# Attention value products with both precision parts in one 512-column pass

## The chip, the cores and the metric

The kernel runs on one core of a Trainium2 chip. Its time is the device time in microseconds (us) of one execution; the time before is the median of three. A profile of one execution shows what each engine did: PE multiplies matrices (a matmul streams the columns of a moving operand past stationary weights, which a separate weight load, PEld, brings in), DVE and ACT do elementwise work and are the only ones here that read PE's results out of PSUM, POOL does elementwise work in SBUF, SP starts transfers. PSUM is cut into banks, and one bank holds 512 float32 columns on 128 partitions.

## The reference

One layer of a hybrid decoder on 1024 tokens of width 1024: RMSNorm, one input projection, 8 heads of causal attention beside 4 heads of a gated recurrence, an output projection, then a gated MLP. What the change touches is the attention:

```python
s = jnp.where(valid[None, :, None, None], s, -jnp.inf)
m = jnp.max(s, axis=-1)
p = jnp.exp(s - m[..., None])
l = jnp.sum(p, axis=-1)
o = jnp.einsum('bnqrhe,...', p.astype(v.dtype), vw)   # weights times values
...
return (num / den[..., None])[:, :S]
```

The three dilation patterns are merged into one softmax per query with an additive mask, so each head is a causal attention of 1024 queries by 1024 keys with 64 columns per head.

## The kernel before, in words

Products at float32 accuracy are made of several products in fp32r: each operand x is split into a high part hi (a rounding copy) and a low part lo = x - hi, and hi*hi, hi*lo and lo*hi are added up in PSUM.

The attention stage runs from about 57 to 298 us. It goes through heads h = 0 to 7, in each through query pairs j = 0 to 3 (256 queries, two blocks A and B of 128), and in each through key pairs i = 0 to j (256 keys). Scores (`score_steps`): PE makes a score bank S of up to 512 keys (L585, L586, two buffers), DVE adds the mask and takes it out into P with the row's minimum (L588), ACT takes the exponential with the row's sum (L593), DVE the reciprocal (L594), POOL scales P (L597). Where a row has more than 512 keys, L592 joins the two minima on DVE. Values (`value_steps`): `tr` transposes four 128x128 blocks of P into one bank T (L612 to L619, two buffers; three blocks on the diagonal, i = j), ACT copies T to the high part (L623), DVE makes the low part from T (L624). `pv` multiplies: the stationary operand is the value tile v with the 64 high columns and the 64 low columns of V beside each other, so that rows 0 to 63 of the result O hold the products with V's high part and rows 64 to 127 those with its low part; the moving operand is the high, then the low part of the transposed weights. That makes four matmuls per tile, two for each block of 128 keys, all adding into columns 0 to 255 of one bank. `end` adds the two halves of the rows: ACT copies rows 64 to 127 to `ot` (L639), DVE adds rows 0 to 63 (L641). There are 48 full tiles and 32 diagonal ones, and 32 ends.

PE's order is written out by the program (the engine is scheduled by hand). Beside the attention it does projection work in portions that `Fill` hands out: the next head's q and k (`qk_half`, products `p__qk`), then value and recurrence projections (`pV`, `piv`). The evacuation of q and k is on DVE (`x`, L549, then L552, L553, L555) and ACT (L550, L551). The order of DVE, ACT and POOL is chosen by a scheduler at build time from its own costs; only instructions given to `pin` keep their program order among each other, and the sums in `end` are among these. Each engine works its own queue strictly in order, so an instruction that waits holds up all behind it.

## Time and profile before

| | |
|---|---|
| median of three runs | 1208.58 us (1207.88 to 1208.98) |
| the profiled execution's own time | 1207.86 us |
| its span in the profile | 1205.9 us |
| PE busy | 1192.7 us, 99% of the span, 6014 matmuls |
| PE weight loads | 1005.6 us, 83% |
| DVE, ACT, POOL busy | 947.8 (79%), 631.4 (52%), 298.5 us (25%) |
| chain that ended last | PE 95%, DVE 3%, ACT 1% |

A busy share says how full an engine is on average; which wait ends last is read in the timeline of the place. The profile gives each matmul a duration that runs over into the following ones, because matmuls are pipelined: steps between starts, not durations, say what PE's time costs. TensorE's granted clock was at full speed in the stretches shown below.

### The profile page before, as it was taken

To read this page: it belongs to the slowest core of one execution; us is meant where nothing else is said; L and a number is where in the kernel's file an instruction comes from. 1 tells how busy PE (TensorE), PEld (TensorE's weight loads), DVE (VectorE), ACT (ScalarE), POOL (GpSimd) and SP (SyncE) were. 2 spreads that over 40 slices of the span, in tenths; PEclk is the share of its full clock that TensorE was granted. 3 is DMA by queue.
4 is the path that set the end of the run, shared out by engine and by line. 5 is a ranking of instruction groups with operands and counts; after the bars stand their busy time and mean duration, and the time that the engine had idled before them with its cause. 6 is when DMAs were issued, how large, how long until landed. Compare 5 with 4: busy or idle time off the path is not lost.

```text
span 1205.9 us, 17474 instructions
## 1 busy us (share of the span) xinstructions
PE 1192.7 (99%) x6014; PEld 1005.6 (83%) x6014; DVE 947.8 (79%) x1783; ACT 631.4 (52%) x1217; POOL 298.5 (25%) x276
## 2 busy tenths in 40 slices
PE   9999999999999999999999999999999999999996
PEld 8988888888888888888888888888888888888886
DVE  8767776666778776484999899898888978957986
ACT  8766666667666565454643343433443444444553
POOL 1154446544001014413231322312223200000000
PEclk9999999999999999999999999999999999999999
DMA  7021112223111123432113323333223267534532
GB/s 273 10 71 54 53 54 88 64 65 120 36 36 54 60 64 112 133 125 94 42 64 114 108 85 106 121 116 109 84 98 122 96 213 249 156 98 158 166 103 89
DMA packets 71833, 122.39 MB, mean 101 GB/s; under 512 B 7360, under 2 KB 17856, under 8 KB 71744
## 3 DMA queue, kind: packets, MB, share of 16 engines
q1 hardware_dynamic: 60528, 101.41, 26.3%
q10 hardware_dynamic: 11216, 19.86, 4.3%
q8 instruction: 47, 0.77, 0.3%
q14 instruction: 42, 0.34, 0.1%
HBM read 97.65 MB, written 23.59 MB: 101 GB/s over the span
## 4 chain that ended last, share of the span: by engine, by line
PE 95%; DVE 3%; ACT 1%; issue 0%; POOL 0%; DVEq 0%; ACTq 0%
PE p L1132 11%; PE p L1133 11%; PE p L1134 11%; PE ds L1433 3%; PE ds L1431 3%; PE ds L1432 3%; PE po L1036 2%; PE po L1038 2%; PE po L1037 2%; PE da L1433 2%; PE da L1431 2%; PE da L1432 2%; PE piv L512 1%; PE piv L514 1%; PE piv L513 1%; PE S L585 1%
## 5 line engine op out<-in xcount | busy, mean ns | idle before, releaser
L88 POOL TENSOR_TENSOR wlo<-raww,whi 128x512 fp32r<-128x512 f32 x141 | 208.6, 1491 | 382.4 <-ACT whi L86 231.6
L86 ACT CAST whi<-raww 128x512 fp32r<-128x512 f32 x276 | 167.7, 617 | 183.9 <-DVE raww L120 69.1
L88 DVE TENSOR_TENSOR wlo<-raww,whi 128x512 fp32r<-128x512 f32 x136 | 97.5, 717 | 22.8 <-ACT whi L86 22.7
L86 ACT CAST whi<-r 128x512 fp32r<-128x512 f32 x70 | 43.6, 623 | 83.1 <-PE ds L1432 51.3
L597 POOL TENSOR_SCALAR P<-P,st 128x512 f32<-128x512 f32 (+2 forms) x96 | 55.8, 592 | 107.9 <-DVE st L594 50.5
L588 DVE CUSTOM_DVE_ANT_0 P<-S,mask 128x512 f32<-128x512 f32 (+2 forms) x96 | 52.0, 553 | 29.9 <-PE S L586 28.9
L593 ACT ACTIVATE P<-P,st 128x128 f32<-128x128 f32 (+3 forms) x64 | 49.7, 777 | 32.0 <-DVE st L588 16.7
L88 DVE TENSOR_TENSOR wlo<-r,whi 128x512 fp32r<-128x512 f32 x70 | 47.9, 685 | 20.0 <-ACT whi L86 19.9
L624 DVE TENSOR_TENSOR tl<-T,th 128x512 fp32r<-128x512 f32 (+1 forms) x80 | 50.8, 634 | 16.2 <-ACT th L623 15.1
L1433 PE MATMUL ds<-fhi,wlo 128*128 128x512 f32 x160 | 62.3, 389 | 0.0
L1432 PE MATMUL ds<-flo,whi 128*128 128x512 f32 x160 | 62.3, 389 | 0.0
L1431 PE MATMUL ds<-fhi,whi 128*128 128x512 f32 x160 | 62.2, 389 | 0.0
L1132 PE MATMUL p<-b1h,whi 128*128 128x512 f32 x160 | 62.2, 389 | 0.0
L1133 PE MATMUL p<-b1l,whi 128*128 128x512 f32 x160 | 62.2, 389 | 0.0
L1134 PE MATMUL p<-b1h,wlo 128*128 128x512 f32 x160 | 62.2, 389 | 0.0
L1161 ACT ACTIVATE cv<-cv 128x512 f32<-128x512 f32 x44 | 27.9, 633 | 61.5 <-DVE cv L1154 61.4
L1154 DVE SCALAR_TENSOR_TENSOR cv<-g,vec,cv 128x511 f32<-128x511 f32 (+2 forms) x92 | 56.1, 615 | 4.7 <-ACT cv L1151 3.7
L1405 POOL TENSOR_TENSOR facc<-facc,sqf 128x256 f32<-128x256 f32 x2 | 1.5, 738 | 223.7 <-ACT sqf L1404 223.7
L623 ACT CAST th<-T 128x512 fp32r<-128x512 f32 (+1 forms) x80 | 43.0, 537 | 23.4 <-PE T L616 20.3
L86 ACT CAST fhi<-rawf 128x512 fp32r<-128x512 f32 x70 | 43.2, 617 | 15.2 <-DMA rawf<-spT 7.0
L88 DVE TENSOR_TENSOR flo<-rawf,fhi 128x512 fp32r<-128x512 f32 x70 | 47.9, 684 | 3.6 <-ACT fhi L86 3.6
L1431 PE MATMUL da<-fhi,whi 128*128 128x512 f32 x120 | 46.7, 389 | 0.0
(672 smaller groups left out, 3832.5 us busy)
## 6 DMA issues: line engine op xcount, KB each, us to landing
raww<-in_w_up_dram SPq DMA_DIRECT2D x88, 256.0 KB, 3.1
raww<-in_w_tok_dram SPq DMA_DIRECT2D x52, 256.0 KB, 2.7
rawf<-spT SPq DMA_DIRECT2D x40, 256.0 KB, 2.7
r<-in_w_down_dram SPq DMA_DIRECT2D x40, 256.0 KB, 3.5
raww<-in_w_hg_dram SPq DMA_DIRECT2D x32, 256.0 KB, 2.6
raww<-in_w_out_dram SPq DMA_DIRECT2D x32, 256.0 KB, 2.6
spB<-a ACTq DMA_DIRECT2D x30, 256.0 KB, 2.2
spT<-t ACTq DMA_DIRECT2D x30, 256.0 KB, 2.0
```

What stands on the lines that cost most here:

```text
L86: self.pin(self.high(hi[:, :w], raw))
L88: self.pin(low.tensor_sub(lo[:, :w], raw, f32(hi[:, :w])))
L588: DVE.tensor_tensor_reduce(Pt[:, k0 : k0 + w], S[:, :w], mask[:, m : m + w], -1.0, BIG * 3, op0=ALU.add, op1=ALU.min, accum_out=st[:, k0 / ...
L597: POOL.tensor_scalar(e, e, st[:, 3:4], 1.0, op0=ALU.mult, op1=ALU.mult)
L624: DVE.tensor_sub(tl[:, :n], T[:, :n], f32(th[:, :n]))
L1132: PE.matmul(ps, hi[:, s], bhi, start=(start and n == 0), stop=False)
L1133: PE.matmul(ps, hi[:, s], blo, start=False, stop=False)
L1134: PE.matmul(ps, lo[:, s], bhi, start=False, stop=(stop and n == len(rhs) - 1))
L1154: DVE.scalar_tensor_tensor(dst, x, col(V_CW + j * NFF + f), dst, op0=ALU.mult, op1=ALU.add)
L1431: PE.matmul(ps[d], hi[:, s], ahi, start=(k == 0), stop=False)
L1432: PE.matmul(ps[d], hi[:, s], alo, start=False, stop=False)
L1433: PE.matmul(ps[d], lo[:, s], ahi, start=False, stop=(k == NPAIR - 1))
```

## The change

High and low part of the transposed weights now lie in one tile `t` of shape 128 x 2 x 512. `pv` streams the two parts in one pass: a moving operand of two runs of 256 columns, one from each part, into a bank seen as two halves, so that the high part's products land in columns 0 to 255 and the low part's in 256 to 511. On the diagonal the second key block goes with two runs of 128 columns into columns 128 to 255 and 384 to 511. A tile takes two matmuls where it took four; the columns that are streamed stay the same. `end` adds three things: ACT copies rows 64 to 127 of the first half as before, DVE adds rows 0 to 63 of the second half to `ot`, then rows 0 to 63 of the first half. The rows 64 to 127 of the second half (low part of V times low part of the weights) are left out of the sum, where the kernel before had them in it. Two early weight tiles that borrow the tags of `th` and `tl` borrow the new one.

```diff
--- before.py
+++ after.py
@@ -369,7 +369,8 @@
     TB = 3
 
     def aside(i):
-        return tuple(at.tile([P, H2], F32R, tag=x, name=f"{x}w{i}", bufs=TB) for x in ("th", "tl"))
+        t = at.tile([P, 2, H2], F32R, tag="t", name=f"tw{i}", bufs=TB)
+        return t[:, 0], t[:, 1]
 
     ring.aside = {(("qk", 1), i): aside for i in range(2)}
     ring.aside["a12", 1] = None
@@ -618,26 +619,27 @@
                 else:
                     PE.transpose(T[:, 256:384], B[:, k1], ident)
                     n = 384
-                th = at.tile([P, H2], F32R, tag="th", name=f"th{h}_{j}_{i}", bufs=TB)
-                tl = at.tile([P, H2], F32R, tag="tl", name=f"tl{h}_{j}_{i}", bufs=TB)
-                ACT.copy(th[:, :n], T[:, :n])
-                DVE.tensor_sub(tl[:, :n], T[:, :n], f32(th[:, :n]))
-                parts[i] = th, tl
+                t2 = parts[i] = at.tile([P, 2, H2], F32R, tag="t", name=f"t{h}_{j}_{i}", bufs=TB)
+                ACT.copy(t2[:, 0, :n], T[:, :n])
+                DVE.tensor_sub(t2[:, 1, :n], T[:, :n], f32(t2[:, 0, :n]))
 
             def pv(i):
-                th, tl = parts.pop(i)
+
+                t2 = parts.pop(i)
                 last = i == j
                 v0, v1 = V[:, 2 * i, h % 4, :], V[:, 2 * i + 1, h % 4, :]
-                PE.matmul(O[:, 0:256], v0, th[:, 0:256], start=(i == 0), stop=False)
-                PE.matmul(O[:, 0:256], v0, tl[:, 0:256], start=False, stop=False)
-                o_, m_ = (O[:, 0:256], slice(256, 512)) if not last else (O[:, 128:256], slice(256, 384))
-                PE.matmul(o_, v1, th[:, m_], start=False, stop=False)
-                PE.matmul(o_, v1, tl[:, m_], start=False, stop=last)
+                o2 = O.rearrange("p (x q) -> p x q", x=2)
+                PE.matmul(o2, v0, t2[:, :, 0:256], start=(i == 0), stop=False)
+                if last:
+                    PE.matmul(o2[:, :, 128:256], v1, t2[:, :, 256:384], start=False, stop=True)
+                else:
+                    PE.matmul(o2, v1, t2[:, :, 256:512], start=False, stop=False)
 
             def end():
                 ot = at.tile([64, 256], F32, tag="ot", name=f"ot{h}_{j}", bufs=2)
                 ACT.copy(ot, O[64:128, 0:256])
                 r0 = 64 * (h % 2)
+                pin(DVE.tensor_add(ot, O[0:64, 256:512], ot))
                 pin(DVE.tensor_add(raw[h // 2, j // 2][r0 : r0 + 64, (j % 2) * 256 : (j % 2 + 1) * 256], O[0:64, 0:256], ot))
 
             for i in range(j + 1):
```

The build-time scheduler also orders DVE, ACT and POOL anew. Two places on DVE are shown, each before and after. In the names, a trailing number is a tile's serial number; `ot_3` and `raw_1` belong to the end of query pair 3 of the head before, `ot_0` and `raw_0` to that of pair 0; `P_6` is the row block 6 of the scores with its two evictions.

The first place is DVE in head 3, from the split of the next head's q and k to the evictions of row block 6. Before:

```order
L592 TENSOR_TENSOR st_5_1889<-st_5_1889 128x1
L553 SCALAR_TENSOR_TENSOR qs_1894<-x_0_1896,qs_1894 64x512
L555 TENSOR_TENSOR kl_204<-x_0_1896,kh_1895 64x512
L594 RECIPROCAL st_5_1889<-st_5_1889 128x1
L641 TENSOR_TENSOR raw_1_562<-O_3_1687,ot_3_1923 64x256
L624 TENSOR_TENSOR tl_1_1_1931<-T_1_1_1926,th_1_1_1930 128x384
L641 TENSOR_TENSOR raw_0_561<-O_0_1835,ot_0_1950 64x256
L588 ISA P_6_1953,st_6_1954<-S_6_0_1955,mask 128x512
L588 ISA st_6_1954 128x1
```

After:

```order
L556 TENSOR_TENSOR kl_202<-x_0_1815,kh_1814 64x512
L595 RECIPROCAL st_5_1808<-st_5_1808 128x1
L642 TENSOR_TENSOR ot_3_1840<-O_3_1621,ot_3_1840 64x256
L624 TENSOR_TENSOR t_1_1_1848<-T_1_1_1844,t_1_1_1848 128x384
L643 TENSOR_TENSOR raw_1_560<-O_3_1621,ot_3_1840 64x256
L642 TENSOR_TENSOR ot_0_1865<-O_0_1758,ot_0_1865 64x256
L589 ISA P_6_1869,st_6_1870<-S_6_0_1871,mask 128x512
L589 ISA st_6_1870 128x1
L643 TENSOR_TENSOR raw_0_559<-O_0_1758,ot_0_1865 64x256
L589 ISA P_6_1869,st_6_1870<-S_6_512_1875,mask 128x384
```

Ahead of the first eviction of `P_6` stood two sums (`raw_1`, `raw_0`); now three stand there (`ot_3`, `raw_1`, `ot_0`), and the fourth (`raw_0`) between the two evictions.

The second place is DVE in head 2, near the end of row block 7, with the evacuation `x_1` of the next head's projection. Before:

```order
L588 ISA st_7_1588 128x1
L592 TENSOR_TENSOR st_7_1588<-st_7_1588 128x1
L594 RECIPROCAL st_7_1588<-st_7_1588 128x1
L624 TENSOR_TENSOR tl_2_1_1618<-T_2_1_1612,th_2_1_1617 128x512
L549 TENSOR_TENSOR x_1_1645<-p__qk___3_1_1509,R_89 128x512
L641 TENSOR_TENSOR raw_0_561<-O_1_1481,ot_1_1634 64x256
L624 TENSOR_TENSOR tl_2_2_1642<-T_2_2_1637,th_2_2_1641 128x384
L552 CAST kh_1501<-x_1_1645 64x512
```

After:

```order
L593 TENSOR_TENSOR st_7_1529<-st_7_1529 128x1
L550 TENSOR_TENSOR x_1_1581<-p__qk___3_1_1454,R_89 128x512
L595 RECIPROCAL st_7_1529<-st_7_1529 128x1
L624 TENSOR_TENSOR t_2_1_1556<-T_2_1_1551,t_2_1_1556 128x512
L642 TENSOR_TENSOR ot_1_1570<-O_1_1427,ot_1_1570 64x256
L624 TENSOR_TENSOR t_2_2_1578<-T_2_2_1574,t_2_2_1578 128x384
L643 TENSOR_TENSOR raw_0_559<-O_1_1427,ot_1_1570 64x256
L553 CAST kh_1446<-x_1_1581 64x512
```

The evacuation `x_1` now stands ahead of the reciprocal of row block 7 and of the lo part `t_2_1`, and the sums of pair 1 have grown from one to two. On ACT the copy `ot_3` has moved ahead of the copies that follow `x_0` (L550, L551), and `ot_0` behind a weight cast (L86). On PE nothing is moved but the merged products.

## Rows read from the trace of the kernel before

**Rows 1.** Busy time in the attention stage. Columns: stretch in us and its length, then for PE, weight loads, DVE, ACT and POOL the busy us with the number of instructions, then the granted clock of TensorE as a share of full speed, the share of the DMA engines and GB/s.

```profile
57.00:298.00 241.00, 238.67 (x1473) 210.15 (x1471) 162.38 (x442) 161.61 (x333) 128.50 (x152) 1.00 0.22 68
```

**Rows 2.** Waits of PE from 57 to 300 us, the row of the score products: who waited, for whom, us in total, times, longest.

```profile
PE S L585 <- DVE st L588: 0.8, 2, 0.4
```

**Rows 3.** Groups of instructions by line and shape: the last product of a tile in its two shapes, which tell the full tiles (48) from the diagonal ones (32), and from the view of one line the sum that ends a query pair (duration in ns: least, median, most).

```profile
L635 PE MATMUL O<-tl,v 128*128 128x256 f32 x48 | 13.6, 283 | 0.0
...
L635 PE MATMUL O<-tl,v 128*128 128x128 f32 x32 | 8.8, 275 | 0.0
...
L641 DVE TENSOR_TENSOR raw<-O,ot x32: 396/417/419, 58.7 to 298.7; 64x256 f32<-64x256 f32 x32
```

**Rows 4.** Timeline of PE in head 3 (columns of every timeline: start, us taken, engine, line, instruction, output and inputs, shape, and in brackets an idle time before it with what ended it). What counts is the step from one start to the next, since the ends run over into the next instruction. First a 512-column step; then a diagonal tile (first product at 146.03) up to the second product of the work behind it; then a full tile (first product at 153.58) up to the work behind it.

```profile
145.33 0.40 PE L460 MATMUL p__qk___4_1_1903<-ulo,whi 128*128 128x512 f32 x1
145.56 0.39 PE L461 MATMUL p__qk___4_1_1903<-uhi,wlo 128*128 128x512 f32 x1
...
146.03 0.28 PE L631 MATMUL O<-th,v 128*128 128x256 f32 x1
...
146.43 0.45 PE L458 MATMUL p__qk___4_1_1903<-uhi,whi 128*128 128x512 f32 x1
146.72 0.40 PE L460 MATMUL p__qk___4_1_1903<-ulo,whi 128*128 128x512 f32 x1
...
153.58 0.28 PE L631 MATMUL O<-th,v 128*128 128x256 f32 x1
...
154.06 0.39 PE L458 MATMUL p__qk___4_1_1903<-uhi,whi 128*128 128x512 f32 x1
```

**Rows 5.** The same timeline at the stop of head 3 near 151.9 us: DVE, then ACT, then PE.

```profile
144.81 0.69 DVE L624 TENSOR_TENSOR tl<-T,th 128x512 fp32r<-128x512 f32 x1 [0.64 <-ACT th L623]
...
149.34 0.17 DVE L594 RECIPROCAL st<-st 128x1 f32<-128x1 f32 x1
149.56 0.42 DVE L641 TENSOR_TENSOR raw<-O,ot 64x256 f32<-64x256 f32 x1
150.07 0.56 DVE L624 TENSOR_TENSOR tl<-T,th 128x384 fp32r<-128x384 f32 x1
150.66 0.42 DVE L641 TENSOR_TENSOR raw<-O,ot 64x256 f32<-64x256 f32 x1
151.10 0.69 DVE L588 CUSTOM_DVE_ANT_0 P<-S,mask 128x512 f32<-128x512 f32 x1
...
149.16 0.37 ACT L639 COPY ot<-O 64x256 f32<-64x256 f32 x1
...
150.06 0.37 ACT L639 COPY ot<-O 64x256 f32<-64x256 f32 x1
...
151.86 0.50 PE L585 MATMUL S<-kh,qs 128*128 128x512 f32 x1 [0.38 <-DVE st L588]
```

**Rows 6.** Timeline some 6 us before the end of a head, in head 2: DVE from the reciprocal of row block 7 to the lo part of the fourth query pair's first key pair (131.02), then PE's last product of the next head's projection and the transposes of the fourth pair's third key pair, which take the bank that this lo part has read.

```profile
125.80 0.16 DVE L594 RECIPROCAL st<-st 128x1 f32<-128x1 f32 x1 [1.37 <-ACT P L593]
126.28 0.69 DVE L624 TENSOR_TENSOR tl<-T,th 128x512 fp32r<-128x512 f32 x1 [0.31 <-ACT th L623]
126.88 0.68 DVE L549 TENSOR_TENSOR x<-p__qk___3_1_1509,R 128x512 f32<-128x512 f32 x1
127.48 0.41 DVE L641 TENSOR_TENSOR raw<-O,ot 64x256 f32<-64x256 f32 x1
127.81 0.54 DVE L624 TENSOR_TENSOR tl<-T,th 128x384 fp32r<-128x384 f32 x1
...
131.02 0.69 DVE L624 TENSOR_TENSOR tl<-T,th 128x512 fp32r<-128x512 f32 x1
...
125.62 0.40 PE L461 MATMUL p__qk___3_1_1509<-uhi,wlo 128*128 128x512 f32 x1
...
131.81 0.28 PE L612 MATMUL T<-ident,P 128*128 128x128 f32 x1
```

**Rows 7.** Timeline, the like places of other heads: the score products at 121, 182 and 282 us, the transposes at 102 and 193 us, then DVE's second score eviction of row block 6 in head 7 (281.68), and the place of rows 6 in head 5 (the transposes on PE, the lo part on DVE).

```profile
101.52 0.33 PE L612 MATMUL T<-ident,P 128*128 128x128 f32 x1
...
121.37 0.50 PE L585 MATMUL S<-kh,qs 128*128 128x512 f32 x1
...
182.19 0.50 PE L585 MATMUL S<-kh,qs 128*128 128x512 f32 x1
...
192.56 0.33 PE L612 MATMUL T<-ident,P 128*128 128x128 f32 x1
...
281.82 0.50 PE L585 MATMUL S<-kh,qs 128*128 128x512 f32 x1
...
282.39 0.40 PE L585 MATMUL S<-kh,qs 128*128 128x512 f32 x1
...
281.68 0.55 DVE L588 CUSTOM_DVE_ANT_0 P<-S,mask 128x384 f32<-128x384 f32 x1
...
227.05 0.27 PE L612 MATMUL T<-ident,P 128*128 128x128 f32 x1
...
225.89 0.67 DVE L624 TENSOR_TENSOR tl<-T,th 128x512 fp32r<-128x512 f32 x1
```

**Rows 8.** Two groups from the view of one line, in the later recurrence stage: L892 streams the same 64 columns twice over (a moving operand in two runs), L891 streams 128 columns in one run. Durations in ns: least, median, most.

```profile
L892 PE MATMUL psA<-E,B x64: 272/273/323, 327.1 to 475.7; 128*64 128x128 f32 x64
...
L891 PE MATMUL psA<-E,B x64: 272/273/324, 327.1 to 475.7; 128*64 128x128 f32 x64
```

## The prediction

> **What bounds the kernel now.** I began with the busy times: PE is at 99% of the span, and in the attention stage, the only stretch that the change touches, at 238.67 of 241 us, with DVE at 162.4, ACT at 161.6 and POOL at 128.5 [rows 1]. The reader sees one full engine, so time that PE saves is time saved, but only where nothing else makes PE late. So I read PE's waits next: those of the score products for DVE add up to just 0.8 us, in two places [rows 2]. That view lists only clear idle time. The timeline shows more: the same score product, the first of row block 7, starts late in each of heads 1 to 4 and in head 7, after the step before it or with a duration of 0.50 instead of 0.40 us [rows 5, 7]. It needs the bank that DVE's eviction of row block 6 has just left, and DVE comes to that eviction through a run of work without gaps from 144.81 on [rows 5]. A second place is nearly as tight: the transposes at 131.81 us take the bank that a lo part left at 131.02 + 0.69 = 131.71, and at 101.52 and 193 us they even start with a small wait (0.33 instead of 0.28 us) [rows 6, 7]. Last I compared how the two programs stand on each engine, to see what DVE has in front of those two places now.
>
> **PE's saving.** A full tile's four products step from 153.58 to 154.06, 0.48 us [rows 4]. Two products of 512 columns take two steps like that from 145.33 to 145.56, 0.23 each, together 0.46. With starts rounded to 0.01 the gain is 0.01 to 0.02; I take 0.015, and 48 tiles [rows 3] give 0.7 us. On the diagonal the gain is larger, because of the 128-column products: from the first product at 146.03 to the second product of the work behind it, at 146.72, are 0.69 us [rows 4]; less one normal step of 0.23 the tile costs 0.46. Two 128-column products cost almost as much as two of 256 do. After the change it is one product of 512 (0.23) and one of 2 x 128 columns, for which I take half of a full tile's 0.48 / 2, so 0.12: together 0.35, a gain of 0.11. With 32 such tiles [rows 3] that is 3.5 us. Gross gain: 4.2 us. Half as many weight loads belong to the same steps and are not counted again.
>
> What these rows don't show is a matmul that writes PSUM in two separate runs. The nearest are L892 and L891 [rows 8]: one reads its moving columns as two runs of 64, the other as one of 128, and both take 273 ns in the median. So a lower bound of the extra cost is nothing. As an upper bound I take a product of 2 x 128 columns at double its step, 0.24; that is 0.12 more in each of 32. I take nothing, being nearest to rows 8.
>
> On this the Trainium skill speaks against the change: "PSUM — Partial Sum Buffer", section Specifications (TRN2), says that PSUM is made of 8-byte cache lines and that any access pattern that isn't contiguous slows matmuls significantly. Rows 8 show no such slowing on the reading side; no row here shows it on the writing side. By that rule the third rival below would come true; by rows 8 the gain stands.
>
> **What it adds, and where.** One DVE sum more per end, 32 of them at 0.417 us in the median [rows 3], 13.3 us. DVE has 241 - 162 = 79 us free in the stage [rows 1], so most of it is covered by waiting that DVE does anyhow. It costs time only in front of something that PE waits for. ACT's copies are as many and as long as before, and DVE's lo parts have the same shape.
>
> Place one, the score product of row block 7 (heads 1 to 4 and 7, five times). Before, from the reciprocal at 149.34 to the eviction at 151.10 DVE does sum, lo part, sum in 1.76 us [rows 5]. Now a third sum is in front of the eviction, 0.42. ACT's copies put bounds on it: the copy at 149.16 moves forward, which frees 0.4 us there, but the copy at 150.06 stands behind a weight cast now, so the third sum has little chance to start early. Small gaps in the 1.76 us (about 0.1) close. I take +0.35, between 0.1 (the gaps close and the added sum starts early) and 0.84 (both added sums count). Five times: 1.75 us. And the saving that PE makes between the chain's start (144.81, which is set by PE's transposes just before) and the stop is lost in the wait: two diagonal tiles, 0.22, five times 1.1 us. In head 7 the next score product also has almost nothing to spare: it starts at 282.39 and its bank is free at 281.68 + 0.55 = 282.23, 0.16 before [rows 7]; a sum of 0.42 now stands between the two evictions, so 0.25 more. In the other heads projection work lies between the two products, and I give the second no cost.
>
> Place two, the transposes near 131.8 us (heads 1 to 4, four times). The evacuation of the next head's projection now stands in front of the reciprocal and of the lo part before it. Before, DVE sat idle 1.37 us until 125.80 and came to the evacuation at 126.88; now it can't begin it until PE's last product of that projection ends, 125.62 + 0.40 = 126.02, which PE's own saving since the stop before (one diagonal, one full tile) brings to about 125.9; I take 126.0 with the time to notice it. Then come in steps from rows 6: evacuation 0.60, reciprocal 0.1, lo part 0.60, the added sum 0.4, and the old sum 0.4, which stood before the next lo part (127.81) and stands behind it now; then 131.02 - 127.81 = 3.21 and the lo part itself 0.69. That ends at 132.0 where it ended at 131.71: +0.3. PE's saving between the two places, two diagonal and three full tiles, 0.265, is lost as well, since the transposes were already waiting or within 0.1 of it. Four times 0.565: 2.3 us. Bounds: 0 (the idle time takes all of it, then 1.1 is lost at most through the hidden saving) and 0.6 a time.
>
> Heads 5 and 6 have the same place with more to spare: lo part done at 225.89 + 0.67 = 226.56, transposes at 227.05, 0.49 [rows 7]. Two added sums stand ahead of it (0.84) and PE comes some 0.3 earlier, against which DVE has its own idle time; I take 0.2 each, 0.4 us, between 0 and 0.65. Heads 0, 5 and 6 have no stop at place one, and their PE saving counts in full.
>
> **The sum.** -4.2 + 1.75 + 1.1 + 0.25 + 2.3 + 0.4 = +1.6 us. Against the profiled execution's own time, 1207.86 us (span 1205.9 and 2.0 around it), that is 1209.5. The median of the three runs lies 0.7 higher, 1208.58, and there it is 1210.2 us, which I predict. So about three quarters of what PE would gain is never seen or is paid back in DVE's order.
>
> **Rivals.** First, the sums hide entirely: DVE's 79 us free time takes them, and neither place grows. Then only the saving between chain start and stop (1.1) and at the three transposes that already wait (0.8) is lost: -4.2 + 1.9 = -2.3, so 1206.3 us; with nothing lost it would be 1204.4. For it speaks that DVE waits at many places; against it that at the two places it does not wait at all. Chance 0.14, of which 0.09 faster by over 0.2%.
>
> Second, slower: DVE's queue becomes the bound in heads 1 to 4. The mechanism is that of place one in full: the sum between the two evictions delays the second eviction as well as the added one in front, so the second score product waits as in head 7 (0.25 in four heads, 1.0), and place two pays 0.6 instead of 0.3 (1.2), and heads 5 and 6 pay 0.4 instead of 0.2 (0.4). That is +1.6 + 2.6 = +4.2, 1212.8 us. It decides once the chain to the first eviction grows by over 0.42 us, a whole sum. For it: the rest of DVE's order there has been changed too, a lo part now stands ahead of the joined minimum of row block 6. Against it: the projection work between the two score products, and 1.37 us of idle time before place two [rows 6]. Chance 0.22, all slower.
>
> Third, the merged products do not do what they say: the 2 x 128 products step at 0.24. Then 3.8 of the 4.2 are gone, and with them the saving of the diagonal tiles that I count as lost in waits (place one keeps 1.75 and 0.25, place two 0.3 and three full tiles' 0.045 each, heads 5 and 6 0.15 each): -0.4 + 2.0 + 1.4 + 0.3 = +3.3, so 1211.9 us. Chance 0.06.
>
> **Chances and range.** 0.2%, 2.4 us, is about what a measurement of this kernel can tell from no change. My forecast, chance 0.58, means 1207.0 to 1211.5 with the bounds of its terms; it lies within 2.4 us for the most part (0.49), above it with 0.08 and below with 0.01. With the rivals (first 0.09 faster and 0.05 same, second 0.22 and third 0.06 slower) that makes faster 0.10, same 0.54, slower 0.36. The range of 1206.2 to 1213.0 takes in the three rivals' times; outside it are the first rival with nothing lost and waits that I do not foresee.
>
> **What would show it.** Value products: half as many, 512-column ones stepping at 0.23, 2 x 128 at 0.12; a step of 0.24 there proves the third rival. The score product of row block 7 starts in heads 1 to 4 some 0.35 + 0.22 later against PE's work before it, so PE's waits for DVE there go from 0.8 to over 2 us in the view of waits; if they stay, the first rival holds. The transposes near 131.8 wait half a microsecond for a lo part, a row that the waits of before did not have. In the recurrence stage and after it nothing changes but the start. I am wrong if PE's waits do not grow, or if other waits appear: POOL's scaling of row blocks 6 and 7 comes later now too.

## The result, and the profile after

The changed kernel takes 1214.93 us in the median of six runs (1213.87 to 1215.78) where the kernel before takes 1208.55 (1207.88 to 1209.21, six runs): a ratio of 1.005, with a 95% interval of 1.004 to 1.006. It is 6.4 us slower, where the prediction had 1.6 us slower and a range that ends at 1213.0. The profiled execution took 1215.10 us with a span of 1213.2; PE is busy for 1191.5 us of it in 5854 matmuls, 160 fewer than before.

The attention stage now ends at about 305.8 us; up to there ACT and POOL have done as many instructions as before up to 298 [rows 1]:

```profile
57.00:305.80 248.80, 238.23 (x1316) 201.85 (x1316) 177.34 (x475) 161.23 (x333) 129.76 (x152) 0.99 0.21 65
```

The stage is 7.8 us longer, and PE is busy in it for as long as before. It stands still for 10.6 us (248.80 - 238.23), where it stood still for 2.3, and DVE has 15 us more to do. So what was lost is in PE's waits. They are, from 36 to 310 us (who waited, for whom, us in total, times, longest; the last row answers to [rows 2]):

```profile
PE T L613 <- DVE t L624: 4.9, 6, 1.0
PE T L614 <- POOL P L598: 3.9, 4, 2.6
PE S L586 <- DVE st L589: 2.3, 5, 0.6
```

The score products (last row) wait 2.3 us where they waited 0.8. The first row was not there before. The second was there before with two waits; it now holds one of 2.6 us. Before:

```profile
PE T L613 <- POOL P L597: 1.7, 2, 1.1
```

The products themselves did what they should. The group of the added sum (least, median and most in ns) answers to [rows 3], the timeline of PE over a diagonal tile of head 3 to [rows 4]:

```profile
L642 DVE TENSOR_TENSOR ot<-O,ot x32: 396/406/417, 59.1 to 306.5; 64x256 f32<-64x256 f32 x32
```

```profile
150.23 0.40 PE L632 MATMUL O<-t,v 128*128 128x512 f32 x1
150.46 0.28 PE L634 MATMUL O<-t,v 128*128 128x256 f32 x1
150.57 0.40 PE L459 MATMUL p__qk___4_1_1822<-uhi,whi 128*128 128x512 f32 x1
150.81 0.40 PE L461 MATMUL p__qk___4_1_1822<-ulo,whi 128*128 128x512 f32 x1
```

From 150.23 to the second product of the next work at 150.81 are 0.58 us, against 0.69 before: 0.11 less, as worked out. The product of 2 x 128 columns steps 0.11 to 0.12, the one of 2 x 256 columns 0.23 (150.23 to 150.46), the step of a product that writes 512 columns in one run. So writing a bank in two runs costs nothing here. The Trainium skill's "PSUM — Partial Sum Buffer", section Specifications (TRN2), says that any access pattern that isn't contiguous slows matmuls significantly; this trace does not agree, for two runs of 128 or 256 columns in one bank.

Where the time went can be read by laying the two traces side by side: each score product and each transpose of the attention stands at the same place of PE's order in both, and the difference of its starts is what has been lost so far. The last such instruction of head 0's stretch starts at 74.30 us before and at 77.31 now, the last ones of heads 1 to 4, of heads 5 and 6 and of head 7 at 214.99, 274.78 and 294.18 before and at 220.24, 282.53 and 301.96 now; the counting begins with a score product of head 0's first row blocks, at 39.37 before and 39.78 now, ahead of the 57 us from which [rows 1] count. The differences of the differences: **head 0 loses 2.60 us, heads 1 to 4 lose 2.24, heads 5 and 6 lose 2.50, head 7 loses 0.03**, together 7.37 in this execution. The steps of 0.2 us and more among them add up to 10.3, all the smaller ones to -2.9, which is for the most part the products' saving.

**Head 0.** POOL, then PE, each with its row of before (the ones of L597 and L613), then the busy times and the granted clock of TensorE in two stretches of 1 us now (columns as in [rows 1]):

```profile
60.77 1.26 POOL L88 TENSOR_TENSOR wlo<-raww,whi 128x512 fp32r<-128x512 f32 x1 [0.23 <-ACT whi L86]
62.01 1.15 POOL L598 TENSOR_SCALAR P<-P,st 128x512 f32<-128x512 f32 x2
...
60.23 1.15 POOL L597 TENSOR_SCALAR P<-P,st 128x512 f32<-128x512 f32 x2
```

```profile
62.75 0.33 PE L614 MATMUL T<-ident,P 128*128 128x128 f32 x1 [2.61 <-POOL P L598]
...
60.98 0.33 PE L613 MATMUL T<-ident,P 128*128 128x128 f32 x1 [1.14 <-POOL P L597]
```

```profile
64.00:65.00 1.00, 1.00 (x7) 1.00 (x6) 0.74 (x4) 0.27 (x1) 0.00 (x0) 0.53 0.03 10
...
66.00:67.00 1.00, 1.00 (x5) 0.95 (x4) 0.74 (x3) 0.14 (x1) 1.00 (x2) 0.50 0.00 0
```

POOL scales row block 5 (62.01) behind a weight split that stood behind this scaling before, when the scaling started at 60.23. PE stands for 2.61 us where it stood for 1.14, and from about 64.0 to 67.5 us the granted clock is 0.50, the 1.2 GHz level. The prediction had no term for this place.

**Place one**, the stop of head 3 [rows 5], on DVE and PE:

```profile
153.61 0.40 DVE L642 TENSOR_TENSOR ot<-O,ot 64x256 f32<-64x256 f32 x1
...
154.40 0.40 DVE L643 TENSOR_TENSOR raw<-O,ot 64x256 f32<-64x256 f32 x1
154.83 0.41 DVE L642 TENSOR_TENSOR ot<-O,ot 64x256 f32<-64x256 f32 x1
155.17 0.67 DVE L589 CUSTOM_DVE_ANT_0 P<-S,mask 128x512 f32<-128x512 f32 x1
```

```profile
155.90 0.50 PE L586 MATMUL S<-kh,qs 128*128 128x512 f32 x1 [0.44 <-DVE st L589]
```

Three sums are ahead of the eviction, as foreseen. The score product loses 0.05, 0.42, 0.04 and 0.42 us in heads 1 to 4 against its start before, and the two of head 7 lose 0.35 together: 1.3 us in all, where the prediction had 3.1 (0.35 and the lost saving of 0.22, five times, and 0.25). In head 3 DVE comes from the first sum to the eviction in 1.56 us (153.61 to 155.17) with three sums, where it took 1.54 (149.56 to 151.10) with two [rows 5]: the gaps in which it waited for ACT's copies took the third.

**Place two**, head 2 [rows 6], on DVE with the cast of before (L552), then on PE and POOL:

```profile
129.50 0.69 DVE L550 TENSOR_TENSOR x<-p__qk___3_1_1454,R 128x512 f32<-128x512 f32 x1 [1.62 <-PE p__qk___3_1_1454 L462]
...
132.02 1.23 DVE L553 CAST kh<-x 64x512 fp32r<-64x512 f32 x1
135.28 0.69 DVE L624 TENSOR_TENSOR t<-T,t 128x512 fp32r<-128x512 f32 x1
...
128.38 0.60 DVE L552 CAST kh<-x 64x512 fp32r<-64x512 f32 x1
```

```profile
136.02 0.33 PE L613 MATMUL T<-ident,P 128*128 128x128 f32 x1 [0.78 <-DVE t L624]
```

```profile
131.68 1.29 POOL L88 TENSOR_TENSOR wlo<-raww,whi 128x512 fp32r<-128x512 f32 x1
```

The order is the one the prediction went through, from the evacuation at 129.50 to the lo part's end at 135.97. That is 6.47 us, where 132.0 - 126.0 = 6.0 was predicted, and the cast at 132.02 alone is 0.63 longer than the 0.60 that it took before (128.38). POOL's weight split began 0.34 us ahead of it and ends 0.28 ahead of its end. (Before, a split's end already stood beside this cast; with no POOL instruction beside it, it takes 0.42.) The four transposes lose 0.81 to 0.85 us each, 3.3 us.

**Heads 5 and 6**, here head 5, on DVE with the same join before (L592), then on POOL and PE:

```profile
225.37 1.14 DVE L593 TENSOR_TENSOR st<-st 128x1 f32<-128x1 f32 x1
...
218.98 0.20 DVE L592 TENSOR_TENSOR st<-st 128x1 f32<-128x1 f32 x1
```

```profile
224.77 1.72 POOL L88 TENSOR_TENSOR wlo<-raww,whi 128x512 fp32r<-128x512 f32 x1
228.14 1.37 POOL L598 TENSOR_SCALAR P<-P,st 128x512 f32<-128x512 f32 x2 [1.65 <-DVE st L595]
```

```profile
228.89 0.33 PE L614 MATMUL T<-ident,P 128*128 128x128 f32 x1 [0.36 <-POOL P L598]
233.76 0.33 PE L613 MATMUL T<-ident,P 128*128 128x128 f32 x1 [0.99 <-DVE t L624]
```

The join of row block 7's two minima, one element a partition, takes 1.14 us in place of 0.20 and ends at 226.51, with POOL's split (224.77 + 1.72 = 226.49). On it hang ACT's exponential, POOL's scaling at 228.14 and the transposes. Both heads together lose 2.95 us at these transposes, where 0.4 was predicted.

### The profile page after: what moved, and what is told of

The parts are those of the page before. It is cut to its first block, busy times and chain, and to the rows that moved or that the text cites. A ratio compares the mean times of both kernels' runs of the same rounds, so it can differ in the third digit from the quotient of the medians.

```text
span 1213.2 us, 17174 instructions
## 1 busy us (share of the span) xinstructions
PE 1191.5 (98%) x5854; PEld 996.8 (82%) x5854; DVE 962.5 (79%) x1815; ACT 631.8 (52%) x1217; POOL 300.1 (25%) x276
## 4 chain that ended last, share of the span: by engine, by line
PE 90%; DVE 6%; ACT 2%; issue 1%; POOL 0%; DMA 0%; DVEq 0%; SPq 0%; ACTq 0%; POOLq 0%
PE p L1134 10%; PE p L1135 10%; PE p L1136 10%; PE ds L1435 3%; PE ds L1434 3%; PE ds L1433 3%; PE po L1038 2%; PE po L1040 2%; PE po L1039 2%; PE da L1435 2%; PE da L1434 2%; PE da L1433 2%; DVE P L589 2%; PE piv L513 1%; PE piv L515 1%; PE piv L514 1%
## 5 line engine op out<-in xcount | busy, mean ns | idle before, releaser
L86 ACT CAST whi<-raww 128x512 fp32r<-128x512 f32 x276 | 168.0, 617 | 192.9 <-DVE raww L120 62.2
L86 ACT CAST whi<-r 128x512 fp32r<-128x512 f32 x70 | 43.6, 623 | 82.1 <-PE ds L1434 45.9
L624 DVE TENSOR_TENSOR t<-T,t 128x512 fp32r<-128x512 f32 (+1 forms) x80 | 50.3, 633 | 10.6 <-ACT t L623 9.7
L623 ACT CAST t<-T 128x512 fp32r<-128x512 f32 (+1 forms) x80 | 43.0, 538 | 27.7 <-PE T L617 25.0
L86 ACT CAST fhi<-rawf 128x512 fp32r<-128x512 f32 x70 | 43.1, 616 | 15.0 <-DMA rawf<-spT 6.5
```

Of the source, the lines that this page charges most:

```text
L86: self.pin(self.high(hi[:, :w], raw))
L624: DVE.tensor_sub(t2[:, 1, :n], T[:, :n], f32(t2[:, 0, :n]))
```

## The experiments

Two theories stood at the start: that the build's new order of DVE, ACT and POOL loses the time (order theory), or that 13.3 us of added DVE work lose it in any order (work theory). An order can be held by itself: a table gives the place of each of the attention's instructions on DVE, ACT and POOL, and each is tied behind the one ahead of it. The kernels that have such a table have higher line numbers; names tell what is what. PE's order is the same in all.

```diff
+    for a, b in zip(seq, seq[1:]):
+        tc.add_manual_dep(b, a.name, mybir.DependencyInfo(
+            mybir.DependencyClass.NoSync, mybir.DependencyReason.DATA), reason="in_order")
```

Times are given against the kernel before, measured in the same session.

**Run 1: the changed kernel in the old order.** Edit: the table of the kernel before in the changed kernel.

> The changed kernel, with the attention's instructions of DVE, ACT and POOL held in the kernel before's order (each added sum stands right ahead of the old one); TensorE's order is untouched. The order theory (the loss is the build's new order on the three engines around the added sum): the 3.0 us in head 0 and the 2.95 us in heads 5 and 6 go, of the 3.3 us at the transposes of heads 1 to 4 about half stays, the 1.3 us at row block 7's score product stays, the products' saving of 4 us stays: 1208.5 - 4 + 1.3 + 1.6 = about 1207.5 us. The work theory (32 sums of 0.41 us cost what they cost in any order): 1214 to 1215 us, as the changed kernel.

Measured: 1212.95 us against 1208.86, +4.1; ratio 1.0035 (1.0021 to 1.0049).

**Run 2: the kernel before in the new order.** Edit: the table of the changed kernel in the kernel before.

> The kernel before, with its own products and sums, and the attention's instructions of DVE, ACT and POOL held in the changed kernel's order (the added sums are simply absent). The order theory: head 0 +3.0, heads 5 and 6 +2.95 and a part of the 3.3 us in heads 1 to 4, together 6 to 8 us: 1214.5 to 1216.5 us. The work theory: 1208.5 us, since no work is added.

Measured: 1214.49 us, +5.6; ratio 1.0048 (1.0035 to 1.0061).

**Run 3: merged products, no added sum, old order.**

```diff
-                pin(DVE.tensor_add(ot, O[0:64, 256:512], ot))
```

> The changed kernel's merged products, without the added sum (so the low parts of the transposed weights do not reach the result), in the kernel before's order. Order theory and work theory alike: the products' saving alone, 3.5 to 4.2 us: 1204.4 to 1205.0 us. A theory that the merged products themselves cost time (two runs of columns in a bank, one tile for both parts): 1208.5 us or more.

Measured: 1206.02 us, -2.8; ratio 0.9976 (0.9968 to 0.9985).

**Run 4: the kernel before with a second sum.**

```diff
+                pin(DVE.tensor_add(raw[...], O[0:64, 0:256], ot))
                 pin(DVE.tensor_add(raw[...], O[0:64, 0:256], ot))
```

> The kernel before, in its own order, with a second sum of the same size right ahead of each old sum (it writes the slice that the old sum then overwrites). The order theory: the 13.3 us of added DVE work are mostly hidden; what shows is row block 7's score product, some 0.3 us in five heads, and up to 0.4 us at the transposes of heads 1 to 4: 1209 to 1211.5 us. The work theory: the changed kernel's loss without its saving, 6.4 + 4 = 10 us: about 1218 us.

Measured: 1214.98 us, +6.1; ratio 1.0051 (1.0039 to 1.0064).

Neither theory holds alone. The products save 2.8 us. The sums cost 6.1 us in the kernel before and 4.1 + 2.8 = 6.9 with merged products, both in the old order. But the order costs as well where no work is added: run 2 came out where the order theory had it, and loses 1.57 us in head 0, 2.05 in heads 1 to 4 and 1.62 in heads 5 and 6. The two overlap, since the changed kernel has both and loses 6.4 us: at place two the new order has the evacuation in front whether or not sums follow, and run 2 loses 0.74 to 0.79 us at each of the four transposes there, nearly what the changed kernel does. PE's waits in the attention, of run 3, of run 1, of run 4 and of run 2:

```profile
PE S L637 <- DVE st L640: 2.3, 5, 0.6
```

```profile
PE S L637 <- DVE st L640: 5.8, 5, 1.2
PE T L664 <- DVE t L675: 3.1, 6, 0.8
```

```profile
PE S L636 <- DVE st L639: 5.0, 5, 1.1
PE T L663 <- DVE tl L675: 1.8, 5, 0.6
```

```profile
PE T L664 <- DVE tl L676: 3.6, 6, 0.7
PE T L665 <- POOL P L649: 3.2, 2, 2.6
```

Run 3 shows where the rest of the products' 4.2 us is: the same score products wait 2.3 us instead of 0.8, so 1.5 us are given back at place one with no sum added. Runs 1 and 4 show the sums: five score products wait 1.2 and 1.0 us each in the mean, and six and five transposes wait for lo parts. In the old order both added sums of the two ends at place one stand ahead of the eviction. So the sums cost at place one, place two and in heads 5 and 6. Are these places the cause, or does a sum cost wherever it stands? Runs 5, 6, 7 and 9 ask that.

**Run 5: all sums of those places moved later.** Edit, shown for head 1 in DVE's order:

```diff
 RECIPROCAL st1_5
-ot0_3<-O0_3,ot0_3
-raw_0_1<-O0_3,ot0_3
 t1_1_1<-T1_1_1,t1_1_1
-ot1_0<-O1_0,ot1_0
-raw_0_0<-O1_0,ot1_0
 P1_6,st1_6<-S1_6_0,mask
...
 st1_6<-st1_6
+ot0_3<-O0_3,ot0_3
+raw_0_1<-O0_3,ot0_3
...
 st1_7<-st1_7
+ot1_0<-O1_0,ot1_0
+raw_0_0<-O1_0,ot1_0
 RECIPROCAL st1_7
...
-ot1_1<-O1_1,ot1_1
-raw_0_0<-O1_1,ot1_1
 t1_2_2<-T1_2_2,t1_2_2
...
 t1_3_0<-T1_3_0,t1_3_0
+ot1_1<-O1_1,ot1_1
+raw_0_0<-O1_1,ot1_1
```

> The changed kernel in the kernel before's order (as in the first run), with both sums of 16 ends moved later on DVE and nothing else: those two ahead of row block 6's eviction (heads 1 to 4 and 7) go behind row block 6's join and ahead of row block 7's reciprocal, that of row pair 1 (heads 1 to 6) goes behind the first low part of row pair 3. The place theory (a sum costs its full 0.42 us where DVE already sets when TensorE goes on, and nothing elsewhere; 16 of the 32 stand in such places): the 4.1 us at row block 7's score products, the 1.7 us at the transposes of heads 1 to 4 and the 1.4 us in heads 5 and 6 go, with them the 0.4 us each that the kernel before waits at row block 7: 1213.0 - 7.2 - 1.5 = about 1204.5 us, within 1204 to 1206. The theory that 13.3 us of added work costs its half wherever it stands: 1212 to 1213 us.

Measured: 1210.60 us against 1209.26, +1.3; ratio 1.0012 (1.0003 to 1.0021).

**Run 6: only those of place one moved.** The first two pairs of the diff above.

> As the run with all sums later, but only the sums ahead of row block 6's eviction (heads 1 to 4 and 7) moved. The place theory: the 4.1 us there go and at most 1.5 us of the kernel before's own waits: 1207.4 to 1208.9 us. The other theory: 1212 to 1213 us.

Measured: 1211.76 us, +2.5; ratio 1.0019 (1.0010 to 1.0028).

**Run 7: the same moves in the kernel before.**

> The kernel before, its products and its one sum an end, in its own order but for the same 16 moves. The place theory: only the waits that it has itself at row block 7's score product go (0.4 us in heads 1 to 4 and some in head 7): 1207.0 to 1207.8 us. The other theory: 1208.5 us.

Measured: 1208.51 us, -0.75; ratio 0.9995 (0.9986 to 1.0004): no difference that can be told.

The first two expectations were too good; run 7's -0.75 is the small end of what the place theory gave it, and not told from nothing. PE's waits of run 5, with DVE's joins of row block 6 and 7 and the reciprocal behind them in head 3, then the waits of run 7 and its join of row block 6, tell why:

```profile
PE T L664 <- DVE t L675: 3.8, 8, 0.7
```

```profile
153.37 0.59 DVE L644 TENSOR_TENSOR st<-st 128x1 f32<-128x1 f32 x1
...
156.65 0.17 DVE L644 TENSOR_TENSOR st<-st 128x1 f32<-128x1 f32 x1
...
158.19 0.16 DVE L646 RECIPROCAL st<-st 128x1 f32<-128x1 f32 x1 [0.59 <-ACT P L645]
```

```profile
PE T L663 <- DVE tl L675: 1.4, 4, 0.6
```

```profile
152.56 0.60 DVE L643 TENSOR_TENSOR st<-st 128x1 f32<-128x1 f32 x1
```

No score product of run 5 waits for DVE any more, but eight transposes do (in run 6 six, 5.4 us), and in run 7, with no work added, four transposes wait that did not wait before. So the two places are one stretch, some 12 us of each of heads 1 to 4 (151.70 to 163.99 us in run 5, with 0.9 us of larger gaps on DVE in all): what makes row block 7's join (156.65) late there makes its exponential on ACT late, the reciprocal behind that, and place two. From the second eviction of row block 6 to this join are 3.39 us in run 5, 2.95 in run 7 and 2.54 before. DVE's idle time ahead of the reciprocal has shrunk from 1.37 us [rows 6] to 0.59, and the sums that were moved into it cost nothing: the reciprocal starts 1.54 or 1.55 us behind the join in all three. That idle time is ACT's exponential; it takes in work that stands behind the join and none of a delay ahead of it.

What makes the join late is not the sums alone. With the sums gone, row block 6's join comes forward to a place beside a weight split on POOL, in heads 1 to 4 of runs 5, 6 and 7 alike, and takes 0.59 or 0.60 us in place of 0.16 (in run 5 the split ends at 153.94, the join at 153.96). That is all of run 7's growth and half of run 5's; the other half is the two sums moved behind it. Moving won back 2.8 of run 1's 4.1 us; what it would win if the join didn't wait for POOL (run 12 shows a form that doesn't) was not run.

**Run 9: second sums only outside these stretches.** Edit: run 4's second sum behind a condition, true for 16 of the 32 ends.

```diff
+                if (h, j) in free:
+                    pin(DVE.tensor_add(raw[...], O[0:64, 0:256], ot))
```

> The kernel before, in its own order, with the second sum of the fourth run only at the 16 ends outside the stretches from row block 6's eviction to the transposes of row pair 3 in heads 1 to 4, the same places in heads 5 to 7 left out too (so 16 of the 32 sums, 6.7 us of DVE work). The theory that DVE sets TensorE's pace in those stretches alone: the 16 sums elsewhere are hidden, 1208.5 to 1209.4 us. The theory that each sum costs some 0.2 us wherever it stands: 6.1 / 2 more, 1211.9 us.

Measured: 1208.76 us against 1208.77, no difference; ratio 1.0001 (0.9992 to 1.0010, so at most 1.2 us). PE's wait at place one is the one of before [rows 2]:

```profile
PE S L636 <- DVE st L639: 0.8, 2, 0.4
```

So 6.7 us of added DVE work show no price, and by difference from run 4 the other 6.7 us cost 6.1. That is the sharpest answer of the study: the price of a sum is its place's.

**Run 10: merged products at these 16 ends alone.** Edit: `pv` and `end` as in the changed kernel where `(h, j) in free`, else four products and one sum.

> The changed kernel in the kernel before's order, with merged products and the added sum only at the same 16 ends, and the four separate products with one sum at the 16 others. The stretch theory: the sums are hidden and more than half of the products' saving of 2.8 us stays, since TensorE is not held up by DVE there: 1206.8 to 1207.8 us, faster than both kernels. The other theory: half the saving and half the cost, 1208.5 - 1.4 + 3.0 = 1210.1 us.

Measured: 1207.99 us, -0.8; ratio 0.9994 (0.9985 to 1.0003). The sign is the expected one, but the interval holds no difference too; this is not a version that can be called faster.

**Run 11: the second half through ACT and POOL.** Half of the work is taken from DVE altogether.

```diff
-                pin(DVE.tensor_add(ot, O[0:64, 256:512], ot))
-                pin(DVE.tensor_add(raw[...], O[0:64, 0:256], ot))
+                ACT.copy(o2, O[0:64, 256:512])
+                pin(DVE.tensor_add(rw, O[0:64, 0:256], o1))
+                POOL.tensor_add(rw, rw, o2)
```

> Merged products at all 32 ends; the second half of the bank is copied by ACT (right behind its copy of the first half's lower rows, 0.37 us) and added to the result by POOL from SBUF, so DVE keeps one sum an end and the kernel before's order. The stretch theory: the run without the added sum (1206.0 us) plus what the ACT copies delay: 1206 to 1207.5 us, faster than both kernels. If ACT or POOL is as tight in those stretches as DVE: the copies stand in the same chains with 0.37 us each and give 1209 to 1212 us.

Measured: 1214.98 us, +6.2; ratio 1.0051 (1.0038 to 1.0063). The second expectation came true and was exceeded. DVE has no instruction more than in run 3, and PE still waits for it. PE's waits, then DVE and POOL at place one of head 3:

```profile
PE T L664 <- DVE t L675: 5.5, 5, 1.6
PE S L637 <- DVE st L640: 5.1, 5, 1.2
```

```profile
153.51 0.42 DVE L697 TENSOR_TENSOR raw<-O,ot 64x256 f32<-64x256 f32 x1 [0.44 <-ACT ot L694]
...
156.32 1.02 DVE L644 TENSOR_TENSOR st<-st 128x1 f32<-128x1 f32 x1
```

```profile
156.03 1.30 POOL L88 TENSOR_TENSOR wlo<-raww,whi 128x512 fp32r<-128x512 f32 x1
```

ACT's copies hold up the sum (0.44), and POOL's additions have pushed a weight split to 156.03, on which the join then stands: 1.02 us for one element a partition. It is the row of head 5 in the changed kernel once more, in four more heads.

**Run 8: POOL's order alone as before.** Edit: a table for POOL only, in the changed kernel; it puts head 0's scaling of row block 5 ahead of the weight split again (the orders differ at one more place, in head 7, where neither kernel loses).

> The changed kernel with POOL's order alone held as before (the scaling of head 0's row block 5 stands ahead of the weight split again; DVE and ACT differ from the changed kernel in two rows). The order theory for head 0: TensorE does not stand 2.6 us at the transposes of row pair 2, its clock does not fall behind that, and the 3.0 us in head 0 go: 1211.5 to 1212.3 us. A rival, that the clock falls there for another reason or the wait comes back at the next transposes: 1213.5 to 1215 us.

Measured: 1212.82 us against 1209.26, +3.6; ratio 1.0030 (1.0019 to 1.0042). The changed kernel has +6.4, so head 0's order is worth 2.8 us. In the trace, head 0's stretch ends 0.40 us early where the changed kernel's ended 2.60 late. PE's wait and the clock of 64 to 68 us:

```profile
61.45 0.33 PE L645 MATMUL T<-ident,P 128*128 128x128 f32 x1 [1.12 <-POOL P L629]
```

```profile
64.00:68.00 4.00, 4.00 (x32) 3.78 (x31) 2.52 (x11) 3.68 (x8) 3.81 (x5) 1.00 0.25 72
```

The wait is that of before again, and the clock stays up.

**Run 12: the join with a scalar in place of a second tensor.**

```diff
-                            DVE.tensor_tensor(st[:, 0:1], st[:, 0:1], st[:, 1:2], op=ALU.min)
+                            DVE.tensor_scalar(st[:, 0:1], st[:, 0:1], st[:, 1:2], 1.0, op0=ALU.min, op1=ALU.mult)
```

> The changed kernel in its own order, with the join of a row block's two minima written as a minimum against a column taken as a scalar, so that DVE reads one tensor from SBUF in place of two. The port theory (a DVE instruction with two tensors in SBUF stands still while POOL runs an instruction that reads SBUF): the joins that took 1.1 us beside POOL's weight splits (rows at 211.5, 225.4, 247.9 and 261.7 us) take 0.2 us, the two waits of 0.36 and 0.34 us for POOL's scaling of row block 7 in heads 5 and 6 go, and the time falls by 0.7 to 1.1 us to 1213.8 to 1214.2 us. The rival (these joins wait for something else, as the eviction ahead of them or the instruction's own form): they stay at 1.1 us, 1214.9 us. The waits of 0.99 and 0.73 us for the low parts in heads 5 and 6 stay under both, since a cast of 1.46 us beside POOL stands ahead of those.

Measured: 1212.99 us against 1208.81, +4.2; ratio 1.0033 (1.0021 to 1.0045), 2.2 us less than the changed kernel's +6.4. The join in the changed kernel and in this one (least, median, most in ns), then in this one the join of row block 7 in head 5 with the weight split that POOL runs meanwhile, and PE's longest wait:

```profile
L593 DVE TENSOR_TENSOR st<-st x32: 139/159/1150, 55.6 to 292.6; 128x1 f32<-128x1 f32 x32
```

```profile
L646 DVE TENSOR_SCALAR st<-st x32: 195/214/216, 55.5 to 288.9; 128x1 f32<-128x1 f32 x32
```

```profile
224.59 0.21 DVE L646 TENSOR_SCALAR st<-st 128x1 f32<-128x1 f32 x1
...
223.99 1.73 POOL L88 TENSOR_TENSOR wlo<-raww,whi 128x512 fp32r<-128x512 f32 x1
```

```profile
PE T L667 <- POOL P L651: 3.2, 2, 2.6
```

All 32 joins take 0.20 to 0.22 us, also the seven that run from start to end while POOL runs a weight split, as the one at 224.59 does (the split runs to 225.72). So it is the second tensor, not the neighbour as such, that made the join wait. Heads 5 and 6 lose nothing now (-0.25 us against before, where the changed kernel lost 2.50). I had expected half of that: the waits for lo parts went too, though the cast of 1.46 us is still there, since cast, split and all else behind the join had come forward with it.

Where the runs won and lost, in us against the kernel before, by the starts of the same PE instructions as in the section on the result (one profiled execution of each, so the sums of the rows differ from the medians by up to some 1 us):

| run | head 0 | heads 1 to 4 | heads 5, 6 | head 7 |
|---|---|---|---|---|
| changed kernel | +2.60 | +2.24 | +2.50 | +0.03 |
| 1: old order | -0.18 | +3.63 | +1.16 | +0.35 |
| 2: before, new order | +1.57 | +2.05 | +1.62 | -0.08 |
| 3: no sum, old order | -0.41 | -0.59 | -0.68 | -0.25 |
| 4: before, second sum | +0.12 | +4.59 | +1.44 | +0.69 |
| 5: sums later | -0.20 | +1.55 | +1.33 | -0.63 |
| 6: place one's sums later | -0.18 | +2.67 | +1.18 | -0.62 |
| 7: before, sums later | -0.01 | +0.25 | 0.00 | -0.45 |
| 8: POOL's order | -0.40 | +2.27 | +2.53 | +0.04 |
| 9: second sums elsewhere | +0.12 | -0.03 | +0.55 | -0.02 |
| 10: merged elsewhere | -0.17 | -0.19 | +0.43 | -0.22 |
| 11: ACT and POOL | -0.14 | +6.62 | -0.01 | +0.21 |
| 12: join by scalar | +2.33 | +2.32 | -0.25 | -0.24 |

The account of the medians, then: merged products -2.8 (run 3); the added sums in the old order +6.9 (run 1 less run 3); head 0's order on POOL +2.8 (the changed kernel less run 8); the rest of the new order -0.5 (run 8 less run 1, within the uncertainty of either), which is a gain of 1.4 in heads 1 to 4 (2.9 at place one, where an old sum now stands behind the eviction, less 1.5 at place two) and a loss of 1.4 in heads 5 and 6. Together +6.4, as differences of a chain of runs must give.

## Why the prediction was wrong

The steps of the sum that failed are head 0, which had no term and lost 2.6 us, and heads 5 and 6, which had 0.4 us and lost 2.95; place two was 1.0 too low. Place one was 1.8 too high, and that luck hid a part of the miss.

**What bounds the kernel.** Right: PE, held up by DVE at place one and place two. The step that was too narrow is that it took them for two places with 1.37 us of DVE idle time between. Runs 5 and 7 show one stretch: a delay of row block 7's join passes through that idle time.

**PE's saving.** Right in its steps: 0.11 less for a diagonal tile, and 0.23 for a product of 512 columns, so 0.46 for a full tile. Of 4.2 us, run 3 leaves 2.8; the prediction had 1.1 lost at place one, the waits show 1.5. The third rival (2 x 128 columns at 0.24) is refuted by the step of 0.11 to 0.12.

**Place one.** Forecast +3.1 with the lost saving, it was 1.3 in the changed kernel. The order was read rightly, three sums ahead of the eviction, but the gaps behind ACT's copies took more of the third than was given them. The upper bound of 0.84 (both added sums count) is what run 4 has in the old order, where five score products wait up to 1.1 us in place of 0.4.

**Place two.** Forecast +2.3, it was 3.3. The term that was mis-sized is the stretch of 3.21 us taken over from rows 6, in which the cast had 0.60 us: it took 1.23 beside a weight split. With that the whole stretch is 0.5 us longer in head 2, more than the 0.26 by which the transposes there lost more than forecast (0.83 for 0.565), so the other terms of this place were somewhat too high; which of them stays open.

**Heads 5 and 6.** The term of 0.4 us (bounds 0 to 0.65) was 2.95. I had counted the added sums there, against 0.49 us to spare. What happened in the changed kernel is another thing: the join moved behind the operations on the projection, next to a weight split of POOL, and took 1.14 us in place of 0.20. Run 12 shows it by taking the second tensor out of the join. (In the old order it is the sums that cost there, 1.26 us in run 4.)

**Head 0.** No term at all. The prediction says in its last sentence that POOL's scaling comes later now, but it never went through POOL's order, on which a weight split had changed places with this scaling. Run 8 puts the price at 2.8 us, more than half of the 4.8 us by which the loss is above the forecast.

**The second rival**, DVE as the bound at full price, 1212.8 us, came closest, in part by luck. Its idea is what runs 1, 4 and 9 show: sums count nearly in full in the stretches and not at all elsewhere. But its largest terms did not come in the changed kernel as it had them: the second score products of heads 1 to 4 start no more than 0.02 us later against the first ones than before, so the projection work between them was a buffer, and nothing in it stands for head 0. What spoke against it wrongly was the idle 1.37 us.

The common fault is in the sum's method: moved instructions were priced with the duration that they had at their old place, and only the engines that the change touches by name were gone through.

## What to carry to other kernels

Work added on an engine with a third of its time free costs its full price in the stretches in which that engine sets the pace, and nothing that shows outside them (0.0 us for 16 sums, and by difference 6.1 for the other 16); a dummy of the added work in the kernel before, first everywhere and then only where the engine has room, tells the two apart at once. When a build decides the order, one more instruction reorders engines that it has nothing to do with, so compare the order of every engine, place by place, and look at what each moved instruction now runs beside. The minimum of two single columns on DVE, written with the second column as a scalar, did not stand behind POOL's weight splits (0.21 us beside one, where it had taken up to 1.15).

## What was not expected of the hardware

Joins that read two columns in SBUF, and the cast from SBUF to SBUF, stand still when they come while POOL runs a weight split: the join took 1.10 and 1.15 us at most in the two kernels in place of 0.16, the cast of 64 x 512 up to 1.47 in place of 0.42 (in heads 5 and 6 of the kernel before as well). The join ends with the split, the cast some 0.3 us behind it. Sums that read one of their tensors from PSUM kept to 0.40 to 0.42 us in the changed kernel. The Trainium skill has the rule in "SBUF — State Buffer", section "SBUF: two separate sides": VectorE and GpSimd share one pair of ports by an exclusive lock that the first to start holds for its whole instruction; on VectorE's side it is asked for by instructions in a mode that uses two ports, and by those with two inputs in SBUF against a GpSimd one that reads SBUF. The traces agree for the joins and casts, down to an instruction of one element a partition. Run 12 shows that the join with its second operand taken as a scalar does not wait.

The stop of 2.61 us in head 0 stands in three records. TensorE's granted clock fell to 0.50, the 1.2 GHz level, from about 64.0 to 67.5 us in the changed kernel, 1.3 us behind the stop's end, and from about 62.0 to 65.4 us in run 12, where the stop ends at 62.66. In run 2 the products behind the same stop keep their full-speed steps (0.23 us for 512 columns), and nothing more is lost than the stop; the granted clock of that record reads 0.95 from end to end. Behind the stop of 1.12 us at that place (run 8) the clock stays at 1.00. So a stop of this length can cost more than its own time, but it doesn't in each execution; what decides stays open. In the changed kernel 1.47 us are the longer stop, and the score products and transposes that start at the low clock and just behind it are 1.5 us later still; the products' saving in head 0 makes the sum 2.60.
